# Moving the second parts of the weights by 64 bytes, and the inputs and gated products to other places, in a two-layer decoder trunk

## The chip, the cores and the metric

The kernel runs on one core of one Trainium2 chip. The metric is the device time of one execution in microseconds (us), as the median of several runs.

## What is computed

The reference is a trunk of two layers over 256 tokens of width 1024, in float32. Each layer adds half a gated feed-forward block (hidden width 2816), a token mixer, and half a second feed-forward block; each block first normalizes its input. The mixer of layer 0 is a pair of gated convolutions, that of layer 1 is attention.

```
x = x + 0.5 * swiglu_ffn(rms_norm(x, ffn1_norm[l]), ffn1_w_gate_up[l], ffn1_w_down[l])
h = rms_norm(x, mix_norm[l])
x = x + (conv_mixers(h, ...) if l % 2 == 0 else dilated_attention(h, ...))
x = x + 0.5 * swiglu_ffn(rms_norm(x, ffn2_norm[l]), ffn2_w_gate_up[l], ffn2_w_down[l])
...
swiglu_ffn: gate, up = split(x @ w_gate_up);  (silu(gate) * up) @ w_down
```

## The kernel before

All activations are kept transposed: 128 channels on the partitions, 256 tokens along the row. The weights come in *units* of 16 tiles of 128x128 float32 (1 MB) in the order of use, into four buffers `raw` of 8 KB a partition (`load`, L111). For more precision than one fast pass gives, each unit is split in two parts (`split`, L117): ScalarE rounds it into `w1` (L126), VectorE subtracts and leaves the rest in `w2` (L127), both in the fast float32 format (`float32r`). `w1` and `w2` have four buffers each. Activations are split in the same way (`split_to`, L183): a normalized input block `xs[:, d]` or a gated product `gs[:, f]` is a first part of 256 columns and a second part of 256 columns.

A tile's product is then formed in one of two ways. `mm2` (L166) issues two matmuls, called a *pair* here: `w1` against both parts at once (512 columns, L168), then `w2` against the first part (256 columns, L169). `mm3` (L158) issues three matmuls of 256 columns, called a *triple* (L162 to L164). Each matmul first loads its own 128x128 weight tile into TensorE.

The work runs in stages, in program order: for each of the four feed-forward blocks 22 gate-up units (`project2`, L324, or `project`, L314; line L375 or L377 of `ffn`), whose results are scaled, gated and split into `gs` (L381 to L388), and then the down products (L400, L402), eight output blocks of 22 tiles; between them the convolution (L422) or the attention (L578). In the feed-forward blocks nearly all tiles take pairs; the last gate-up unit, a few first ones (`ONES`) and the last output block take triples. The convolution and the attention's values and output take triples, the attention's queries and keys pairs. `Norm.add` (L287) writes the next stage's `xs` block by block as the output blocks are finished.

**Places.** A place is an address within a partition, modulo 1024 (`LINE`). A gap at L97 lets the tiles of the pool `keep` begin at a multiple of 1024, and all of `raw`, `w1` and `w2` follow at multiples of 1024. A 128x128 tile takes 512 bytes of a row, so a weight tile begins at place 0 or 512. The moving operand begins at a place that two constants set: `XS_START` for `xs` (288 in both feed-forward blocks of layer 0, 32 in those of layer 1, 192 in the convolution, 256 in the attention) and `GS_START` for `gs` (its tile begins at place 256, in the last block 320, so that 800 and 736 both give place 32). The attention's `o1` begins at place 256. Within `xs` and `gs` the two parts of a block lie side by side, 1024 bytes each, so that the 512 columns of `mm2` are one run of 2048 bytes.

Of the kernel before, what the change touches and what calls it, by code (L numbers as in the profile page):

```python
# [10 lines left out]
F32 = mybir.dt.float32  # L11
F32R = mybir.dt.float32r
# [5 lines left out]
P = 128  # L18
D = 1024
S = 256  # L20
DEPTH = 2
FF = 2816
ND = D // P
NF = FF // P
# [27 lines left out]
ONES = [4, 0, 0, 2]  # L52
ONE_END = 1
PRIO_F = 0
FFN_STEP = 40
# [4 lines left out]
WIDEC = 0  # L60
LINE = 1024
BASE = 16512
XS_START = {"F1": (288, 32), "MX": (192, 256), "F2": (288, 32)}
GS_START = (800, 800, 800, 736)
GROUPS = ((0, 2), (2, 4), (4, 6), (6, 8))
M_POOL = [0, 0, 0, 0]
B_POOL = [0, 0]
# [10 lines left out]
C_F1, C_MX, C_F2, C_FN = 0, DEPTH * ND, 2 * DEPTH * ND, 3 * DEPTH * ND  # L78
# [15 lines left out]
def trunk(ctx: ExitStack, tc: tile.TileContext, xin, wst, cst, bia, idn, out):  # L94
    nc = tc.nc
    keep = ctx.enter_context(tc.tile_pool(name="keep", bufs=1))
    keep.tile([P, (LINE - BASE % LINE) // 4], F32, name="gap")  # L97
    raws = ctx.enter_context(tc.tile_pool(name="raws", bufs=RAWS))
    w1s = ctx.enter_context(tc.tile_pool(name="w1s", bufs=WS))
    w2s = ctx.enter_context(tc.tile_pool(name="w2s", bufs=WS))  # L100
    tmp = ctx.enter_context(tc.tile_pool(name="tmp", bufs=2))
    psa = ctx.enter_context(tc.tile_pool(name="psa", bufs=4, space=PSUM))
    psb = ctx.enter_context(tc.tile_pool(name="psb", bufs=4, space=PSUM))
# [5 lines left out]
    at = {"load": 0, "split": 0}  # L109
# [20 lines left out]
    def advance(u, ahead_split=ahead_split):  # L130
        while at["load"] < min(n_units, u + ahead_load):
            load(at["load"])
            at["load"] += 1
        while at["split"] < min(n_units, u + ahead_split):
            split(at["split"])
            at["split"] += 1
# [3 lines left out]
    whole = {0} | {first_conv + i for i in WHOLE}  # L140

    class Stream:
        def __init__(self, u):
            self.u = u
# [8 lines left out]
    def take(n):  # L153
        st = Stream(used[0])
        used[0] += n
        return st

    def mm3(o, a, b, start, stop, check=False):  # L158
        if len(a) == 1:
            nc.tensor.matmul(o, a[0], b[-1], start=start, stop=stop, skip_group_check=check)  # L160
            return
        nc.tensor.matmul(o, a[0], b[0], start=start, stop=False, skip_group_check=check)  # L162
        nc.tensor.matmul(o, a[0], b[1], start=False, stop=False, skip_group_check=check)  # L163
        nc.tensor.matmul(o, a[1], b[0], start=False, stop=stop, skip_group_check=check)  # L164

    def mm2(o, w, b, start, stop):  # L166

        nc.tensor.matmul(o, w[0], b, start=start, stop=False, skip_group_check=True)  # L168
        nc.tensor.matmul(o[:, 0], w[1], b[:, 0], start=False, stop=stop, skip_group_check=True)  # L169


    x = keep.tile([P, ND, S], F32, name="x")
    xs_all = keep.tile([P, ND * 2 * S + LINE // 4], F32R, name="xs")
    const_all = keep.tile([P, LINE // 4], F32, name="const")
    const = const_all[:, :NCONST]
    ident = keep.tile([P, P], F32, name="ident")
# [6 lines left out]
    def split_to(o1, o2, src, scale=None):  # L183

        if scale is None:
            nc.scalar.copy(o1, src)
            nc.vector.tensor_sub(o2, src, o1.bitcast(F32))
        else:
            nc.scalar.activation(o1, src, AF.Copy, scale=scale)  # L189
            nc.vector.scalar_tensor_tensor(o2, src, scale, o1.bitcast(F32),  # L190
                                           op0=ALU.mult, op1=ALU.subtract)
# [86 lines left out]
    class Norm:  # L278


        def __init__(self, col, whole=None, start=0):
            self.col, self.whole = col, whole
            self.xs = xs_all[:, start // 4:start // 4 + ND * 2 * S].rearrange(
                "p (d t s) -> p d t s", d=ND, t=2)
            self.sums = tmp.tile([P, S], F32, name="sums")

        def add(self, d):  # L287
# [23 lines left out]
    def twice(r):  # L311
        return r[:, None, :].to_broadcast([P, 2, S])

    def project(st, base, xs, xg=None):  # L314

        bank = psa.tile([P, 2, S], F32, name="pa")
        for i in range(2):
            for k in range(ND):
                w = st.tile(base + 2 * k + i)
                b = (xs[:, k, 0], xs[:, k, 1]) if len(w) == 2 else (xg[:, k],)  # L320
                mm3(bank[:, i], w, b, k == 0, k == ND - 1)
        return bank

    def project2(st, base, xs):  # L324

        banks = []
        for i in range(2):
            bank = psa.tile([P, 2, S], F32, name="pa")
            for k in range(ND):
                mm2(bank, st.tile(base + 2 * k + i), xs[:, k], k == 0, k == ND - 1)  # L330
            banks.append(bank)
        return banks

    def join(v, banks, r):

        for i, bank in enumerate(banks):
            h = tmp.tile([P, S], F32, name="sq")
            nc.scalar.copy(h, bank[:, 1])  # L338
            nc.vector.tensor_add(v[:, i], bank[:, 0], h)  # L339
        nc.vector.tensor_mul(v, v, twice(r))  # L340
# [23 lines left out]
    def ffn(norm, after, between=None, first=None):  # L364
        _, r = norm.end(True, first is None)
        with tc.tile_pool(name="gp", bufs=1, reuse_waits="tile") as gp:
            st = take(NF)
            start = GS_START[st.u // FFN_STEP] // 4
            gs = gp.tile([P, NF * 2 * S + start], F32R, name="gs")[:, start:].rearrange(
                "p (f t s) -> p f t s", f=NF, t=2)  # L370
            for p in range(NF):
                advance(st.u + p)
                one = p < ONES[st.u // FFN_STEP] or p >= NF - ONE_END
                if one:
                    bank = first if first and p == 0 else project(st, p * UT, norm.xs)  # L375
                else:
                    banks = project2(st, p * UT, norm.xs)  # L377
                with tc.high_priority(offset=PRIO_F):
                    v = tmp.tile([P, 2, S], F32, name="v")
                    if one:  # L380
                        nc.vector.tensor_mul(v, bank, twice(r))  # L381
                    else:
                        join(v, banks, r)
                    sl = tmp.tile([P, S], F32, name="sl")
                    nc.scalar.activation(sl, v[:, 0], AF.Silu)  # L385
                    g = tmp.tile([P, S], F32, name="g")
                    nc.vector.tensor_mul(g, sl, v[:, 1])
                    split_to(gs[:, p, 0], gs[:, p, 1], g)  # L388
            if between:
                between(gs[:, NF - 1, 0, :1].bitcast(F32))  # L390
            st = take(NF * ND // UT)
            for d in range(ND):
                acc = psb.tile([P, 2, S], F32, name="pb")
                two = d < ND - 1
                for f in range(NF):
                    t = d * NF + f
                    if t % UT == 0 or f == 0:
                        advance(st.u + t // UT)
                    if two:
                        mm2(acc, st.tile(t), gs[:, f], f == 0, f == NF - 1)  # L400
                    else:
                        mm3(acc[:, 0], st.tile(t), (gs[:, f, 0], gs[:, f, 1]), f == 0, f == NF - 1)  # L402
                for i in range(2 if two else 1):
                    nc.vector.scalar_tensor_tensor(x[:, d], acc[:, i], 0.5, x[:, d],  # L404
                                                   op0=ALU.mult, op1=ALU.add)
                after.add(d)

    def out_half(st, accs, half, o, ds, ahead=(ahead_split,) * 2):

        for d in ds:  # L410
            for k in range(4):
                t = half * 32 + d * 4 + k
                if t % UT == 0:
                    advance(st.u + t // UT, ahead[t // UT % 2])
                mm3(accs[d // 2][:, d % 2], st.tile(t), [a[:, k] for a in o],
                    half == 0 and k == 0 and d % 2 == 0, half == 1 and k == 3, True)
# [290 lines left out]
    cold = psb.tile([P, P], F32, name="pb")  # L707
    for _ in range(WARM):
        nc.tensor.matmul(cold, ones, ones, start=True, stop=True)
    norm = Norm(C_F1, start=XS_START["F1"][0])  # L710
    for layer in range(DEPTH):
        nxt = Norm(C_MX + layer * ND, start=XS_START["MX"][layer])
        if layer == 0:
            ffn_first(norm, nxt)
        else:
            ffn(norm, nxt)
        norm, nxt = nxt, Norm(C_F2 + layer * ND, start=XS_START["F2"][layer])
        (conv if layer % 2 == 0 else attention)(norm, nxt)
        if layer < DEPTH - 1:
            norm, nxt = nxt, Norm(C_F1 + (layer + 1) * ND, start=XS_START["F1"][layer + 1])  # L720
            ffn(norm, nxt)
            norm = nxt
    with tc.tile_pool(name="fp", bufs=1, reuse_waits="tile") as fp:
# [7 lines left out]
        for i, (lo, hi) in enumerate(GROUPS):  # L731
            n = hi - lo
# [93 lines left out]
```

## Time and profile before

| | |
|---|---|
| median of 3 runs | 960.75 us (959.98 to 960.87) |
| the profiled execution | 960.66 us |
| its span, first to last instruction | 958.9 us |
| TensorE matmuls busy | 945.5 us, 99% of the span |
| VectorE busy | 724.3 us, 76% |
| ScalarE busy | 543.3 us, 57% |
| DMA | 176.24 MB, mean 184 GB/s |
| mean granted TensorE clock | 0.997 |

The span is the time from the first to the last instruction in the trace; the execution's own time holds 1.8 us more. Matmuls are pipelined, and the trace's duration of one runs on while the next has begun; what the stream of matmuls costs is read from the distance between their starts.

### The profile page before, as it was taken

How to read it: one execution, taken by the hardware profiler on the slowest of the kernel's cores; microseconds unless marked ns; L12 is line 12 of the kernel's file. 1: busy time of each engine (PE TensorE's matmuls, PEld its weight loads, DVE VectorE, ACT ScalarE, POOL GpSimd, SP SyncE). 2: the span in 40 equal slices, each digit the busy share in tenths (PEclk: the TensorE clock that was granted, in tenths of full speed). 3: DMA queues.
4: the chain of work that ended last, by engine and by line, in shares of the span. 5: the costliest groups of instructions: out<-in, count | busy, mean ns of one | idle time of the engine just before them, and what ended most of it. 6: DMA issues, size and time to landing. Idle time of an engine off the chain costs nothing.

```text
span 958.9 us, 15090 instructions
## 1 busy us (share of the span) xinstructions
PE 945.5 (99%) x5828; PEld 845.8 (88%) x5828; DVE 724.3 (76%) x1373; ACT 543.3 (57%) x975; POOL 47.1 (5%) x61
## 2 busy tenths in 40 slices
PE   8999999999999999999999999999999999999996
PEld 7988898999888888988988889898888998889886
DVE  7988866688879878766788877665698798788552
ACT  6666554488265565554466565444676565665541
POOL 0000000049600000000000000000000000000000
PEclk9999999999999999999999999999999999999998
DMA  8855555544176555555455555555553455555501
GB/s 328 291 205 192 178 206 189 178 159 148 45 260 213 193 207 181 180 211 181 176 194 202 176 191 205 178 195 212 195 191 129 149 186 194 194 202 177 194 26 44
DMA packets 27287, 176.24 MB, mean 184 GB/s; under 512 B 3024, under 2 KB 3792, under 8 KB 6864
## 3 DMA queue, kind: packets, MB, share of 16 engines
q1 hardware_dynamic: 26784, 174.67, 51.7%
q8 instruction: 45, 0.74, 0.3%
q10 hardware_dynamic: 432, 0.63, 0.2%
q14 instruction: 26, 0.21, 0.1%
HBM read 174.23 MB, written 1.05 MB: 183 GB/s over the span
## 4 chain that ended last, share of the span: by engine, by line
PE 90%; POOL 3%; DVE 3%; ACT 1%; DMA 1%; issue 1%; SPq 0%; DVEq 0%; POOLq 0%; ACTq 0%
PE pa L168 33%; PE pa L169 17%; PE pb L168 15%; PE pb L169 8%; PE pa L162 4%; PE pa L163 3%; PE pa L164 3%; POOL yp L486 3%; PE pa L160 2%; PE pb L162 1%; PE pb L163 1%; PE pb L164 1%; DVE pb L463 1%; PE pa L352 1%; PE pb L652 1%
## 5 line engine op out<-in xcount | busy, mean ns | idle before, releaser
L127 DVE TENSOR_TENSOR w<-raw,w 128x1024 fp32r<-128x1024 f32 (+1 forms) x316 | 377.0, 1205 | 136.3 <-ACT w L126 135.9
L168 PE MATMUL pa<-xs,w 128*128 128x512 f32 x1376 | 479.4, 391 | 0.1
L126 ACT CAST w<-raw 128x1024 fp32r<-128x1024 f32 (+1 forms) x316 | 320.5, 1032 | 133.5 <-PE pa L168 49.7
L169 PE MATMUL pa<-xs,w 128*128 128x256 f32 x1376 | 387.2, 282 | 0.0
L168 PEld LDWEIGHTS pa<-xs,w 128*128 128x128 f32 x1376 | 258.1, 188 | 54.9 <-DVE xs L190 0.7
L169 PEld LDWEIGHTS pa<-xs,w 128*128 128x128 f32 x1376 | 260.0, 189 | 0.3
L168 PE MATMUL pb<-gs,w 128*128 128x512 f32 x616 | 213.7, 390 | 0.0
L169 PE MATMUL pb<-gs,w 128*128 128x256 f32 x616 | 173.7, 282 | 0.0
L168 PEld LDWEIGHTS pb<-gs,w 128*128 128x128 f32 x616 | 115.6, 188 | 24.1
L169 PEld LDWEIGHTS pb<-gs,w 128*128 128x128 f32 x616 | 116.4, 189 | 0.0
L385 ACT ACTIVATE sl<-v 128x256 f32<-128x256 f32 x88 | 36.8, 418 | 108.7 <-DVE v L340 104.3
L338 ACT COPY sq<-pa 128x256 f32<-128x256 f32 x172 | 62.9, 366 | 28.6 <-PE pa L169 26.1
L163 PE MATMUL pa<-xs,w 128*128 128x256 f32 x272 | 76.3, 281 | 0.1
L162 PE MATMUL pa<-xs,w 128*128 128x256 f32 x272 | 76.3, 282 | 0.0
L164 PE MATMUL pa<-xs,w 128*128 128x256 f32 x272 | 76.2, 281 | 0.0
L339 DVE TENSOR_TENSOR v<-pa,sq 128x256 f32<-128x256 f32 x156 | 65.5, 420 | 0.0
L404 DVE SCALAR_TENSOR_TENSOR x<-pb,x 128x256 f32<-128x256 f32 x60 | 25.4, 423 | 42.5 <-PE pb L169 28.5
L189 ACT ACTIVATE xs<-x,const 128x256 fp32r<-128x256 f32 x48 | 24.3, 506 | 55.2 <-DVE x L404 43.1
L486 POOL TENSOR_TENSOR yp<-yp,prod 128x256 f32<-128x256 f32 x55 | 45.1, 822 | 208.8 <-ACT prod L485 204.8
L340 DVE TENSOR_TENSOR v<-v,rr 128x512 f32<-128x512 f32 x78 | 53.6, 688 | 0.0
L162 PEld LDWEIGHTS pa<-xs,w 128*128 128x128 f32 x272 | 51.4, 190 | 0.3
L163 PEld LDWEIGHTS pa<-xs,w 128*128 128x128 f32 x272 | 51.1, 188 | 0.5 <-DVE xs L190 0.3
(155 smaller groups left out, 900.7 us busy)
## 6 DMA issues: line engine op xcount, KB each, us to landing
raw<-wst SPq DMA_DIRECT2D x159, 1024.0 KB, 4.8
bt<-bia SPq DMA_DIRECT2D x8, 384.0 KB, 3.3
raw<-wst SPq DMA_DIRECT2D x7, 256.0 KB, 6.3
raw<-wst SPq DMA_DIRECT2D x2, 512.0 KB, 5.6
x<-xin SPq DMA_DIRECT2D x3, 256.0 KB, 5.7
out<-y SPq DMA_DIRECT2D x2, 256.0 KB, 2.5
out<-y ACTq DMA_DIRECT2D x2, 256.0 KB, 2.4
x<-xin SPq DMA_DIRECT2D x2, 128.0 KB, 3.2
```

Of the source, the lines that this page charges most:

```text
L126: nc.scalar.copy(w1[u][:, c], raw[u][:, c])
L127: nc.vector.tensor_sub(w2[u][:, c], raw[u][:, c], w1[u][:, c].bitcast(F32))
L162: nc.tensor.matmul(o, a[0], b[0], start=start, stop=False, skip_group_check=check)
L163: nc.tensor.matmul(o, a[0], b[1], start=False, stop=False, skip_group_check=check)
L164: nc.tensor.matmul(o, a[1], b[0], start=False, stop=stop, skip_group_check=check)
L168: nc.tensor.matmul(o, w[0], b, start=start, stop=False, skip_group_check=True)
L169: nc.tensor.matmul(o[:, 0], w[1], b[:, 0], start=False, stop=stop, skip_group_check=True)
L338: nc.scalar.copy(h, bank[:, 1])
L339: nc.vector.tensor_add(v[:, i], bank[:, 0], h)
L340: nc.vector.tensor_mul(v, v, twice(r))
L385: nc.scalar.activation(sl, v[:, 0], AF.Silu)
L486: nc.gpsimd.tensor_add(yp[:, c], yp[:, c], t)
```

## The change

The buffers of `w2` begin 64 bytes past a multiple of 1024, through a gap of 64 bytes before them and one of 960 after them; those of `w1` stay at multiples of 1024. `xs` and `gs` are laid out by a new function `blocks`: all first parts one after the other, then all second parts, each series beginning at a place that is given (the first number of each pair for the first parts, the second for the second parts; they are equal throughout). The tile `xs` grows by 2048 bytes. The places are

| | before | after |
|---|---|---|
| `xs`, feed-forward 1, layers 0 and 1 | 288, 32 | 288, 0 |
| `xs`, convolution, attention | 192, 256 | 192, 256 |
| `xs`, feed-forward 2, layers 0 and 1 | 288, 32 | 16, 192 |
| `gs`, the four feed-forward blocks in order | 32, 32, 32, 32 | 32, 304, 128, 64 |
| `w1` tiles | 0 or 512 | 0 or 512 |
| `w2` tiles | 0 or 512 | 64 or 576 |

`THREE` is empty, so the conditions that use it are what they were. The number, kind and order of the operations in the source are unchanged.

```diff
-XS_START = {"F1": (288, 32), "MX": (192, 256), "F2": (288, 32)}
-GS_START = (800, 800, 800, 736)
+XS_AT = {'F1': ((288, 288), (0, 0)), 'MX': ((192, 192), (256, 256)), 'F2': ((16, 16), (192, 192))}
+GS_AT = ((32, 32), (304, 304), (128, 128), (64, 64))
+GS_BASE = (256, 256, 256, 320)
+THREE = ()
+W_GAP = 64
...
     w1s = ctx.enter_context(tc.tile_pool(name="w1s", bufs=WS))
+    gaps = [ctx.enter_context(tc.tile_pool(name="gap1", bufs=1))]
+    gaps[0].tile([P, W_GAP // 4], F32, name="gap")
     w2s = ctx.enter_context(tc.tile_pool(name="w2s", bufs=WS))
+    gaps.append(ctx.enter_context(tc.tile_pool(name="gap2", bufs=1)))
+    gaps[1].tile([P, (LINE - W_GAP) // 4], F32, name="gap")
...
+    def blocks(t, base, at, n):
+        lo = (at[0] - base) % LINE
+        step = n * S * 4 + (at[1] - at[0]) % LINE
+        a = t[:, lo // 4:(lo + 2 * step) // 4].rearrange("p (t q) -> p t q", t=2)
+        return a[:, :, :n * S].rearrange("p t (k s) -> p k t s", k=n)
...
-    xs_all = keep.tile([P, ND * 2 * S + LINE // 4], F32R, name="xs")
+    xs_all = keep.tile([P, ND * 2 * S + 3 * LINE // 4], F32R, name="xs")
...
-            self.xs = xs_all[:, start // 4:start // 4 + ND * 2 * S].rearrange(
-                "p (d t s) -> p d t s", d=ND, t=2)
+            self.xs = blocks(xs_all, 0, at, ND)
...
-            start = GS_START[st.u // FFN_STEP] // 4
-            gs = gp.tile([P, NF * 2 * S + start], F32R, name="gs")[:, start:].rearrange(
-                "p (f t s) -> p f t s", f=NF, t=2)
+            n = st.u // FFN_STEP
+            gs = blocks(gp.tile([P, NF * 2 * S + 3 * LINE // 4], F32R, name="gs"), GS_BASE[n],
+                        GS_AT[n], NF)
...
-                two = d < ND - 1
+                two = d < ND - 1 and n not in THREE
```

## Rows read from the trace of the kernel before

**Rows 1.** The page's head, busy times, and chain by engine and by line.

```profile
span 958.9 us, 15090 instructions
...
PE 945.5 (99%) x5828; PEld 845.8 (88%) x5828; DVE 724.3 (76%) x1373; ACT 543.3 (57%) x975; POOL 47.1 (5%) x61
...
PE 90%; POOL 3%; DVE 3%; ACT 1%; DMA 1%; issue 1%; SPq 0%; DVEq 0%; POOLq 0%; ACTq 0%
```

**Rows 2.** Busy time in two stretches (us), all engines: gate-up, layer 1; down, layer 0.

```profile
480.00:580.00 100.00, 100.00 (x579) 88.64 (x578) 81.56 (x131) 61.05 (x110) 0.00 (x0) 1.00 0.55 191
410.00:460.00 50.00, 50.00 (x290) 44.34 (x290) 31.55 (x44) 23.09 (x31) 0.00 (x0) 1.00 0.54 190
```

**Rows 3.** Line L168 in single windows: durations ns min/median/max, first and last start.

```profile
L168 PE MATMUL pa<-xs,w x289: 390/390/390, 479.9 to 579.8; 128*128 128x512 f32 x145
L168 PE MATMUL pb<-gs,w x145: 390/390/391, 410.0 to 459.9; 128*128 128x512 f32 x145
```

**Rows 4.** Groups by line and form: the pairs' and triples' counts.

```profile
L168 PE MATMUL pa<-xs,w 128*128 128x512 f32 x1376 | 479.4, 391 | 0.1
L168 PE MATMUL pb<-gs,w 128*128 128x512 f32 x616 | 213.7, 390 | 0.0
L163 PE MATMUL pa<-xs,w 128*128 128x256 f32 x272 | 76.3, 281 | 0.1
L163 PE MATMUL pb<-gs,w 128*128 128x256 f32 x88 | 24.5, 279 | 0.0
L163 PE MATMUL pa<-o,w 128*128 128x256 f32 x64 | 18.4, 288 | 0.0
```

**Rows 5.** Timeline of weight loads and matmuls, gate-up of layer 0.

```profile
100.08 0.39 PE L168 MATMUL pa<-xs,w 128*128 128x512 f32 x1
100.08 0.19 PEld L169 LDWEIGHTS pa<-xs,w 128*128 128x128 f32 x1
100.31 0.28 PE L169 MATMUL pa<-xs,w 128*128 128x256 f32 x1
```

**Rows 6.** Timeline, first and last L162 of three series: down, convolution, attention output.

```profile
460.57 0.28 PE L162 MATMUL pb<-gs,w 128*128 128x256 f32 x1
467.92 0.28 PE L162 MATMUL pb<-gs,w 128*128 128x256 f32 x1
228.27 0.28 PE L162 MATMUL pa<-xs,w 128*128 128x256 f32 x1
231.80 0.28 PE L162 MATMUL pa<-xs,w 128*128 128x256 f32 x1
751.98 0.28 PE L162 MATMUL pa<-o,w 128*128 128x256 f32 x1
755.94 0.28 PE L162 MATMUL pa<-o,w 128*128 128x256 f32 x1
```

**Rows 7.** Timeline, L168 in two steps of the attention's queries and keys.

```profile
687.50 0.40 PE L168 MATMUL pa<-xs,w 128*128 128x512 f32 x1
692.45 0.40 PE L168 MATMUL pa<-xs,w 128*128 128x512 f32 x1
704.41 0.39 PE L168 MATMUL pa<-xs,w 128*128 128x512 f32 x1
707.53 0.39 PE L168 MATMUL pa<-xs,w 128*128 128x512 f32 x1
```

**Rows 8.** Groups by line and form: VectorE over 1024, 512 and 256 columns.

```profile
L127 DVE TENSOR_TENSOR w<-raw,w 128x1024 fp32r<-128x1024 f32 x304 | 368.4, 1223 | 133.6 <-ACT w L126 133.2
L340 DVE TENSOR_TENSOR v<-v,rr 128x512 f32<-128x512 f32 x78 | 53.6, 688 | 0.0
L187 DVE TENSOR_TENSOR gs<-g,gs 128x256 fp32r<-128x256 f32 x88 | 36.8, 419 | 0.0
```

**Rows 9.** Timeline, layer 1: the first down matmul, the last gated product's second part.

```profile
590.90 0.39 PE L168 MATMUL pb<-gs,w 128*128 128x512 f32 x1
595.03 0.42 DVE L187 TENSOR_TENSOR gs<-g,gs 128x256 fp32r<-128x256 f32 x1
```

More of the change, by code (lines that the diff above doesn't have):

```diff
@@ L278, in trunk, with __init__ @@
     class Norm:
-        def __init__(self, col, whole=None, start=0):
+        def __init__(self, col, whole=None, at=(0, 0)):
             self.col, self.whole = col, whole
-            self.xs = xs_all[:, start // 4:start // 4 + ND * 2 * S].rearrange(
-                "p (d t s) -> p d t s", d=ND, t=2)
+            self.xs = blocks(xs_all, 0, at, ND)
             self.sums = tmp.tile([P, S], F32, name="sums")
@@ L367, in ffn @@
             st = take(NF)
-            start = GS_START[st.u // FFN_STEP] // 4
-            gs = gp.tile([P, NF * 2 * S + start], F32R, name="gs")[:, start:].rearrange(
-                "p (f t s) -> p f t s", f=NF, t=2)
+            n = st.u // FFN_STEP
+            gs = blocks(gp.tile([P, NF * 2 * S + 3 * LINE // 4], F32R, name="gs"), GS_BASE[n],
+                        GS_AT[n], NF)
             for p in range(NF):
                 advance(st.u + p)
-                one = p < ONES[st.u // FFN_STEP] or p >= NF - ONE_END
+                one = n in THREE or p < ONES[n] or p >= NF - ONE_END
                 if one:
@@ L709, in trunk @@
         nc.tensor.matmul(cold, ones, ones, start=True, stop=True)
-    norm = Norm(C_F1, start=XS_START["F1"][0])
+    norm = Norm(C_F1, at=XS_AT["F1"][0])
     for layer in range(DEPTH):
-        nxt = Norm(C_MX + layer * ND, start=XS_START["MX"][layer])
+        nxt = Norm(C_MX + layer * ND, at=XS_AT["MX"][layer])
         if layer == 0:
@@ L716, in trunk @@
             ffn(norm, nxt)
-        norm, nxt = nxt, Norm(C_F2 + layer * ND, start=XS_START["F2"][layer])
+        norm, nxt = nxt, Norm(C_F2 + layer * ND, at=XS_AT["F2"][layer])
         (conv if layer % 2 == 0 else attention)(norm, nxt)
         if layer < DEPTH - 1:
-            norm, nxt = nxt, Norm(C_F1 + (layer + 1) * ND, start=XS_START["F1"][layer + 1])
+            norm, nxt = nxt, Norm(C_F1 + (layer + 1) * ND, at=XS_AT["F1"][layer + 1])
             ffn(norm, nxt)
```

## The prediction

> **What bounds the kernel now.** Look first at the page's head and its chain of waits: matmuls are busy for 99% of the span, and 90% of the chain that ends last is TensorE [rows 1]. The busy share alone says little, because a matmul's recorded duration (390 ns) runs on under the next one; what counts is the distance between starts. So look next at the busy times of a long stretch of gate-up and one of down: no idle TensorE time, a granted clock of 1.00 (the upper of its two levels, 2.4 GHz), VectorE busy for 81.56 of 100 us, ScalarE for 61.05, DMA for 0.55 of its share [rows 2]. Nothing feeds TensorE too slowly there. The stream of matmuls sets the time by itself.
>
> Its pace is read from the first and last start of line L168 in those windows: (579.8 - 479.9) / 288 = 0.3469 us from pair to pair in gate-up, (459.9 - 410.0) / 144 = 0.3465 us in down [rows 3]. I call it 346.7 ns. There are 1376 + 616 = 1992 pairs [rows 4], so 1992 x 346.7 ns = 690.6 us of the span of 958.9 us are pairs at this pace, some 72%. A change that moves the pair by 1 ns moves the time by 2.0 us. The triples are 272 + 88 + 64 = 424.
>
> The last view is the timeline inside a pair: the 512-column matmul starts, the load of the next weight tile starts with it, and the 256-column matmul follows after 0.23 us, which leaves about 0.117 us for that one [rows 5]. So **each weight load reads its 512 bytes of a row while the matmul before it reads its moving operand**. The change touches only this: at which places the two read.
>
> **What the trace says of places.** Triples are the same three instructions of the same sizes in three stages. With `gs` at place 32 a triple takes (467.92 - 460.57) / 21 = 350.0 ns, with `xs` at 192 (231.80 - 228.27) / 10 = 353.0 ns, with `o1` at 256 (755.94 - 751.98) / 11 = 360.0 ns [rows 6]. The weights are at 0 or 512 each time. That is 116.7, 117.7 and 120.0 ns a matmul: a spread of 3.3 ns that goes with the place, though the trace alone can't exclude what else differs between the stages. Pairs show the same size of step in another way: in the attention, with `xs` at 256, one step runs at (692.45 - 687.50) / 14 = 353.6 ns a pair and another at (707.53 - 704.41) / 9 = 346.7 ns [rows 7]. The pace of a pair thus has two observed levels 6.9 ns apart, 3.4 ns a matmul, and at 256 the place alone doesn't choose between them.
>
> **The change part by part.**
>
> *The second parts of the weights 64 bytes on.* No instruction is added or taken away. In a pair, one load of two (that of `w2`, under the 512-column matmul) is at a new distance from the moving operand. The load of `w1`, under the 256-column matmul, keeps its distance wherever `xs` or `gs` keeps its place. The trace has no load at a distance of 64 from the others. Bounds from the nearest rows: a gain or a loss of one level for the whole pair, 6.9 ns x 1992 = 13.7 us either way [rows 4, 7]; nothing in the rows excludes either sign. I take half a level, 3.4 ns of one matmul in each pair, as a gain: 1992 x 3.4 = 6.8 us less. The sign comes from the series of triples, in which the pace falls as the distance from the weights' place falls (360.0 at 256, 353.0 at 192, 350.0 at 32 [rows 6]); moving the load towards the operand shortens that distance where it is positive, as at 288, 304, 192, 128 and 256. Where it becomes negative (places 0, 16, 32), no row tells, and I carry the same value over. This is the weakest step.
>
> *Other places of inputs and gated products.* The feed-forward stages that move are the gate-up of the second (288 to 16), third (32 to 0) and last block (32 to 192), and the down of the second to fourth (32 to 304, 128, 64). The trace has 288 and 32 side by side only in pairs, at the same recorded durations of 390 ns; 192 and 256 only in triples or in the attention. The nearest triples bound it at 0 to +1.0 ns a matmul (32 to 192) and +3.3 ns at the worst (256) [rows 6]; a gain is not excluded, since neither 0 nor 64 is measured. Value: 0.
>
> *Two runs instead of one.* The 512 columns of a pair's first matmul become two runs of 256, 8 KB apart in `xs` and 22 KB in `gs`. No row has a matmul of two runs. Below, it costs nothing, if the pattern's second dimension is free. Above, it is like two matmuls of 256: 2 x 116.7 = 233.4 ns instead of 346.7 - 117 = 229.7, so 3.7 ns x 1992 = 7.4 us [rows 3, 4, 6]. I take 0, as no new weights are loaded between the two runs.
>
> *Triples.* 424 at a level's share of at most 3.3 ns a matmul: 424 x 3 x 3.3 = 4.2 us either way, taken as 0, for in a triple only one load of three moves.
>
> *The splitting on VectorE and ScalarE.* `w2` is now written at another place than `raw` and `w1` are read at. VectorE takes 1223 ns for 1024 columns, 688 for 512, 419 for 256 [rows 8]: 535 ns for the upper 512 columns and 269 for 256, the same 1.05 ns a column whatever is read and written. So no price of equal places is there to be saved. Were the new place dearer by 10%, VectorE would add some 122 ns to each of about 36 splits in 100 us, 4.4 us on 81.56 [rows 2]: hidden under TensorE. The cover would go only if VectorE passed 100.
>
> *Sum.* -6.8 us and zeros, from the profiled execution's own 960.66 us (span 958.9 and 1.8 around it, 0.09 below the median): 953.9 us, say **954**. A faster pair is not given back: at 343.3 ns, VectorE's 81.56 becomes 82.4 in 100 us, and DMA has half its share left [rows 2].
>
> **The rivals.**
>
> *Nothing changes, 960.7 us.* The loads and the moving operand don't disturb each other, and the spread in the triples comes from the stages. For it: at places 288 and 32 the pairs have equal recorded durations. Against it: 350.0 and 360.0 for the same instructions at the same clock [rows 6]. The Trainium skill's page "TensorE: Matmul & The Clock Gate", in "Part 2: What happens when you issue a matmul", has a rule on this side: TensorE has two independent read ports, so that loading the next weights takes no read bandwidth from the running matmul. By that rule the whole change is worth 0 and the sum is 960.7. The triples bear it out only if a cause other than place is found for them.
>
> *Both loads gain, 947 us.* If the new distance puts the pair one full level lower, it is 13.7 us: 960.66 - 13.7 = 947.0. For it: a level is the step that the pairs show [rows 7]. Against it: only one load of two moves, and no row has pairs below 346.
>
> *The slow level in the feed-forward blocks, 974 us.* If `w2` at 64 brings the attention's 353.6 ns into all pairs, it is 1992 x 6.9 = 13.7 us more: 974.4; with half of the stages, 967.5. It decides from a third of the pairs on: 664 x 6.9 = 4.6 us lost there cancel 1328 x 3.4 = 4.5 us gained on the others. For it: the level exists [rows 7]. Against it: the long stretches at 32 hold 346.7 over 288 pairs without a slip [rows 3].
>
> *A wait at the four down stages, 979 us.* The first down matmul starts at 590.90, while the last gated product's second part is written until 595.03 + 0.42 = 595.45 [rows 9]. It may start because it reads only block 0. Its operand now spans from block 0's first part across all other first parts to block 0's second part. If the wait that is set for it covers this whole span, TensorE idles for 4.55 us at each of four starts: 18.2 us, 978.9. Behind the waiting matmul stands the whole queue of TensorE. Against it: what it reads overlaps nothing that is still to be written.
>
> **How the numbers follow.** Half a level faster (954, its own range 950 to 958): 0.42. A full level (947): 0.20. Nothing: 0.19. The slow level in part or all (967 to 974): 0.14. The wait: 0.05. Faster by over 0.2% (1.9 us, about what a measurement of this kernel can tell from no change): 0.42 + 0.20 = 0.62; within it 0.19; slower 0.14 + 0.05 = 0.19. The range from 945 to 966 takes in both gains with 2 us of slack, no change, and the two runs at their upper price on top of half a level (954 + 7 = 961) or most of it on top of no gain (968); it leaves out most of the slow level and the wait, about 0.18.
>
> **What would show it.** Right: the distance of L168's starts in the same two kinds of stretch falls from 346.7 to about 343, the 512-column matmul alone being shorter (below 0.23 us), with VectorE's 1223 ns unchanged. The rivals: 340 for the full level, 346.7 for nothing, 353 for the slow one; for the wait, idle TensorE time of 4.5 us ahead of the first L168 on `gs`, released by L187. The prediction is wrong in its cause if the time falls while pairs keep 346.7, or if the 256-column matmul is the one that changes in a stage whose `xs` keeps its place (the first gate-up, at 288).

## The result, and the profile after

The changed kernel takes 967.39 us (966.55 to 967.74 over three runs), against 960.75: a ratio of 1.0062, 95% interval 1.0044 to 1.0080. It is slower by 0.6%, where 954 and faster had been forecast. The profiled execution took 967.74 us, with this head, busy times and chain (from the page):

```profile
span 966.0 us, 15090 instructions
...
PE 952.1 (99%) x5828; PEld 845.6 (88%) x5828; DVE 723.8 (75%) x1373; ACT 543.1 (56%) x975; POOL 47.1 (5%) x61
...
PE 92%; ACT 3%; DVE 2%; POOL 1%; DMA 1%; issue 0%; SPq 0%; DVEq 0%; POOLq 0%; ACTq 0%
```

As in [rows 1] TensorE fills the span, with the same number of instructions. The two long stretches, gate-up of layer 1 and down of layer 0, read like [rows 2]: no idle time, the granted clock 1.00, the other engines about as busy as before.

```profile
485.00:585.00 100.00, 100.00 (x578) 88.41 (x578) 80.61 (x130) 61.09 (x111) 0.00 (x0) 1.00 0.57 197
415.00:465.00 50.00, 50.00 (x289) 43.74 (x289) 31.22 (x43) 22.88 (x31) 0.00 (x0) 1.00 0.55 188
```

No new wait explains the time: the matmuls themselves take longer. The groups by line and form say which (L183 is L168 of before, L184 is L169, L134 is L127):

```profile
L183 PE MATMUL pa<-xs,w 128*128 128x512 f32 x1376 | 482.5, 394 | 0.0
L184 PE MATMUL pa<-xs,w 128*128 128x256 f32 x1376 | 385.3, 280 | 0.0
L183 PE MATMUL pb<-gs,w 128*128 128x512 f32 x616 | 215.6, 394 | 0.0
L134 DVE TENSOR_TENSOR w<-raw,w 128x1024 fp32r<-128x1024 f32 x304 | 367.8, 1221 | 138.8 <-ACT w L133 138.3
```

The 512-column matmul's mean goes from 391 and 390 to 394 ns [rows 4]; VectorE's split stays where it was, 1221 against 1223 ns [rows 8]. A mean over all stages hides the pattern, which appears stage by stage. Here is line L183 in one window for each of the eight feed-forward stages, in order, and last the attention (count, duration min/median/max in ns, first and last start in us; the count at the end of a row is that of a sample):

```profile
L183 PE MATMUL pa<-xs,w x257: 389/393/398, 34.7 to 124.0; 128*128 128x512 f32 x129
L183 PE MATMUL pb<-gs,w x154: 389/393/397, 132.1 to 185.5; 128*128 128x512 f32 x154
L183 PE MATMUL pa<-xs,w x287: 390/394/400, 299.7 to 399.7; 128*128 128x512 f32 x144
L183 PE MATMUL pb<-gs,w x153: 393/397/403, 409.3 to 463.0; 128*128 128x512 f32 x153
L183 PE MATMUL pa<-xs,w x289: 391/392/393, 484.8 to 584.7; 128*128 128x512 f32 x145
L183 PE MATMUL pb<-gs,w x154: 391/392/394, 594.1 to 647.2; 128*128 128x512 f32 x154
L183 PE MATMUL pa<-xs,w x284: 392/392/393, 784.8 to 884.8; 128*128 128x512 f32 x142
L183 PE MATMUL pb<-gs,w x154: 393/395/396, 893.0 to 946.5; 128*128 128x512 f32 x154
L183 PE MATMUL pa<-xs,w x127: 391/392/498, 678.9 to 734.8; 128*128 128x512 f32 x127
```

Last minus first start, over the count less one, is the pace of a pair: (884.8 - 784.8) / 283 = 353 ns in the seventh line, (584.7 - 484.8) / 288 = 347 in the fifth. The table takes the same from the trace's starts in nanoseconds, over the pairs alone and with those that hold a stall left out, as sums of the mean distance behind the 512-column matmul and that behind the 256-column one. The paces that the expectations below quote differ from these by up to 0.7 ns.

| stage | pairs | place before, after | ns a pair before | after | us |
|---|---|---|---|---|---|
| gate-up 1 | 272 | 288, 288 | 228.4 + 118.3 = 346.7 | 230.9 + 118.0 = 348.9 | +0.6 |
| down 1 | 154 | 32, 32 | 228.3 + 118.3 = 346.7 | 230.8 + 118.1 = 348.9 | +0.3 |
| gate-up 2 | 336 | 288, 16 | 228.5 + 118.3 = 346.8 | 232.3 + 117.7 = 350.0 | +1.1 |
| down 2 | 154 | 32, 304 | 228.3 + 118.3 = 346.7 | 232.6 + 120.8 = 353.3 | +1.0 |
| gate-up 3 | 336 | 32, 0 | 228.4 + 118.3 = 346.7 | 229.7 + 117.1 = 346.7 | 0.0 |
| down 3 | 154 | 32, 128 | 228.3 + 118.3 = 346.7 | 229.6 + 117.1 = 346.7 | 0.0 |
| gate-up 4 | 304 | 32, 192 | 228.4 + 118.3 = 346.7 | 231.7 + 121.6 = 353.3 | +2.0 |
| down 4 | 154 | 32, 64 | 228.3 + 118.3 = 346.7 | 232.0 + 118.0 = 350.0 | +0.5 |
| attention | 128 | 256, 256 | 234.2 + 116.5 = 350.8 | 229.6 + 117.1 = 346.7 | -0.5 |

The pairs make +5.1 us of the 6.6 (sums are rounded). The attention's 96 value matmuls of 512 columns go from 227.5 to 232.2 ns, +0.5 us, and the 424 triples, by their starts, add some +0.7 us; the rest is within the spread of the runs. The first two stages are the telling ones: their places did not move, so only the gap acts there, and only on the matmul under which `w2` is loaded.

The wait that was feared at the down stages isn't there. The timeline at the third down has its first matmul on `gs` right behind the last gate-up matmul, as in [rows 9]:

```profile
594.03 0.28 PE L179 MATMUL pa<-xs,w 128*128 128x256 f32 x1
594.15 0.39 PE L183 MATMUL pb<-gs,w 128*128 128x512 f32 x1
```

### The profile page after: what moved, and what is told of

It reads as the page before. It is cut to its first block, busy times and chain, and to the rows that moved or that the text cites. A ratio compares the mean times of both kernels' runs of the same rounds, so it can differ in the third digit from the quotient of the medians.

```text
span 966.0 us, 15090 instructions
## 1 busy us (share of the span) xinstructions
PE 952.1 (99%) x5828; PEld 845.6 (88%) x5828; DVE 723.8 (75%) x1373; ACT 543.1 (56%) x975; POOL 47.1 (5%) x61
## 4 chain that ended last, share of the span: by engine, by line
PE 92%; ACT 3%; DVE 2%; POOL 1%; DMA 1%; issue 0%; SPq 0%; DVEq 0%; POOLq 0%; ACTq 0%
PE pa L183 33%; PE pa L184 17%; PE pb L183 15%; PE pb L184 8%; PE pa L177 4%; PE pa L179 4%; PE pa L178 4%; PE pa L175 3%; ACT prod L499 2%; PE pb L177 1%; PE pb L178 1%; PE pb L179 1%; DVE pb L477 1%; POOL yp L500 1%; ACT w L133 1%; PE pb L666 1%
## 5 line engine op out<-in xcount | busy, mean ns | idle before, releaser
L183 PE MATMUL pa<-xs,w 128*128 128x512 f32 x1376 | 482.5, 394 | 0.0
L134 DVE TENSOR_TENSOR w<-raw,w 128x1024 fp32r<-128x1024 f32 (+1 forms) x316 | 376.4, 1203 | 141.6 <-ACT w L133 141.1
L184 PE MATMUL pa<-xs,w 128*128 128x256 f32 x1376 | 385.3, 280 | 0.0
L183 PEld LDWEIGHTS pa<-xs,w 128*128 128x128 f32 x1376 | 258.3, 188 | 58.6 <-DVE xs L205 0.4
L184 PEld LDWEIGHTS pa<-xs,w 128*128 128x128 f32 x1376 | 259.2, 188 | 0.2
L183 PE MATMUL pb<-gs,w 128*128 128x512 f32 x616 | 215.6, 394 | 0.0
L184 PE MATMUL pb<-gs,w 128*128 128x256 f32 x616 | 173.0, 281 | 0.0
L183 PEld LDWEIGHTS pb<-gs,w 128*128 128x128 f32 x616 | 116.0, 188 | 26.6
L184 PEld LDWEIGHTS pb<-gs,w 128*128 128x128 f32 x616 | 115.7, 188 | 0.0
L178 PE MATMUL pa<-xs,w 128*128 128x256 f32 x272 | 76.6, 282 | 0.0
L178 PEld LDWEIGHTS pa<-xs,w 128*128 128x128 f32 x272 | 51.2, 188 | 0.4 <-DVE xs L205 0.2
```

Of the source, the lines that this page charges most:

```text
L134: nc.vector.tensor_sub(w2[u][:, c], raw[u][:, c], w1[u][:, c].bitcast(F32))
```

## The experiments

Sixteen runs followed: twelve kernels derived from the changed one, and four repeats. A ratio is that to the kernel before, timed beside it on the same chip; where none is given the kernel ran once. *Distance* is the place of the moving operand less that of the weight tile (0 for `w1`, the gap for `w2`).

**1 to 4: the change taken apart.** Each edit is against the changed kernel.

e1_layout, the layout alone:

```diff
-    ...gap1, gap2...
-XS_AT = {... (288, 288), (0, 0) ... (16, 16), (192, 192)}
+XS_AT = {... (288, 288), (32, 32) ... (288, 288), (32, 32)}
-GS_AT = ((32, 32), (304, 304), (128, 128), (64, 64))
+GS_AT = ((32, 32), (32, 32), (32, 32), (32, 32))
```

> The new layout in two runs (all first parts, then all second parts), with every place as in the kernel before and no gap: weights at 0 or 512, xs at 288, 192, 288, 32, 256, 32, gs at 32. Theory (the pace of the pairs follows the places alone): as the kernel before, 346.7 ns a pair in all feed-forward stages, 960.7 us, within 1 us. Rival (the 512 columns in two runs cost something): the 512-column matmul goes from 228 ns up by up to 3.7 ns in every stage, the time to between 962 and 968 us.

Measured: 960.58 us, ratio 0.9993 (0.9985 to 1.0002). The 512 columns in two runs cost nothing; every feed-forward stage runs at 346.7 to 346.8 ns, as the window of the third gate-up shows, which is [rows 3] again (L178 is L168):

```profile
L178 PE MATMUL pa<-xs,w x290: 390/390/390, 479.7 to 579.9; 128*128 128x512 f32 x145
```

e2_gap, the same with the gap of 64 kept:

```diff
-XS_AT, GS_AT of the change
+XS_AT, GS_AT of e1_layout
```

> The new layout and the 64 bytes before the second parts of the weights, with xs and gs at the places of before. Theory: the first gate-up (288) and the first down (32) of the changed kernel, whose places did not move, ran at 349.0 ns a pair, so all eight feed-forward stages run at 349.0 here, 2.3 ns x 1864 pairs = 4.3 us more than before, while the attention's pairs gain 4 ns x 128 = 0.5 us as in the changed kernel: about 964.5 us. Rival (the gap is harmless, the new places of xs and gs cost all): 960.7 us.

Measured: 965.35 us, ratio 1.0045 (1.0033 to 1.0058). All eight feed-forward stages run at 348.9 ns, 230.8 + 118.1: the whole loss sits in the matmul under which `w2` is loaded. Third gate-up, and second down:

```profile
L183 PE MATMUL pa<-xs,w x287: 389/393/397, 479.9 to 579.7; 128*128 128x512 f32 x144
L183 PE MATMUL pb<-gs,w x153: 389/393/397, 410.6 to 463.6; 128*128 128x512 f32 x153
```

(579.7 - 479.9) / 286 = 349 against 347 of e1: the expectation holds in size, stage and matmul, and the rival falls. The 230.8 is a mean: from pair to pair the distance behind this matmul is 226, 231 and 235 ns in turn, through each of the eight stages, where it was 228 or 229 almost throughout before. The attention gained less than expected (348.5, though its places and gap are those of the changed kernel, which had 346.7).

One rival is VectorE, which now writes `w2` at another place while TensorE reads. Its share differs between the two windows, 81% in the gate-up and 63% in the down:

```profile
480.00:580.00 100.00, 100.00 (x575) 87.58 (x575) 81.21 (x138) 59.66 (x109) 0.00 (x0) 1.00 0.54 186
411.00:461.00 50.00, 50.00 (x289) 43.81 (x288) 31.56 (x45) 23.52 (x33) 0.00 (x0) 1.00 0.55 192
```

The pace is 348.9 ns in both, so it doesn't follow VectorE's load.

e3_places, the new places without the gap:

```diff
-    ...gap1, gap2...
```

> The new layout and the new places of xs and gs, without the gap (second parts of the weights at 0 or 512 like the first). Theory that only the distance between a weight load and the moving operand counts: the first gate-up, the first down and the attention, whose places are those of before, return to 346.7 ns a pair (346.7 to 353 in the attention); the others take a pace of their own, not that of the changed kernel, as each load of w2 is 64 bytes nearer. If gap and places added up, the time would be 960.7 + (967.4 - 964.5) = 963.6 us. Rival (the gap alone costs): 960.7 us.

Measured: 965.84 us, ratio 1.0048 (1.0036 to 1.0061). The places alone cost as much as the gap alone, and the two together (1.0062) cost less than their sum: they don't add up, because each decides what the other does. First gate-up and first down are back at 346.7. At gap 0 the place 128 takes 351.0 ns, where at gap 64 it took 346.7; 304 takes 349.9 instead of 353.3, and 64 takes 353.2 instead of 350.0; 192 takes 353.2 and 16 takes 346.9. The rows are the fourth gate-up (192) and the third down (128):

```profile
L178 PE MATMUL pa<-xs,w x284: 397/397/398, 784.8 to 884.8; 128*128 128x512 f32 x142
L178 PE MATMUL pb<-gs,w x152: 387/396/400, 593.9 to 646.9; 128*128 128x512 f32 x152
```

One thing fits no theory of the places: the convolution, whose places are those of e1_layout, ran its triples at 341.9 ns here (113.7 + 113.8 + 114.4) and at 352.2 there. In equal windows of 23 us, the second matmul of a triple, first e1_layout, then e3_places:

```profile
L173 PE MATMUL pa<-xs,w x66: 281/281/281, 220.9 to 243.9; 128*128 128x256 f32 x66
...
L173 PE MATMUL pa<-xs,w x68: 276/276/276, 221.0 to 243.8; 128*128 128x256 f32 x68
```

e4_shift, every distance of before at another place:

```diff
+    ...gap1 ahead of w1s, so that w1 and w2 both begin at 64...
+XS_AT = {'F1': ((352, 352), (96, 96)), 'MX': ((256, 256), (320, 320)), 'F2': ((352, 352), (96, 96))}
+GS_AT = ((96, 96), (96, 96), (96, 96), (96, 96))
```

> Both parts of the weights 64 bytes past a multiple of 1024, and xs and gs 64 bytes further than in the kernel before (352, 96, 256, 320; gs 96): every distance between a weight load in the split format and the moving xs or gs is that of before, every place is another. Theory (distance counts): 346.7 ns a pair in all feed-forward stages, 960.7 us within 1 us. Rival (the place itself counts, as that of xs against something that didn't move with it): paces between 347 and 353 ns as at the other places of the changed kernel, 963 to 973 us.

Measured: 960.70 us, ratio 0.9993 (0.9984 to 1.0002). The paces of all eight feed-forward stages come back to within 0.1 ns of the kernel before: with this shift at least, the distance between the weight load and the moving operand counts, not the place. Third gate-up and second down, beside [rows 3]:

```profile
L183 PE MATMUL pa<-xs,w x290: 390/390/390, 479.6 to 579.8; 128*128 128x512 f32 x145
L183 PE MATMUL pb<-gs,w x154: 390/390/390, 410.7 to 463.8; 128*128 128x512 f32 x154
```

The attention's `o1` stayed at 256 and so changed its distance: its triples went from 120 to 115 ns a matmul.

**5 to 8: sweeps.** Four kernels with other gaps and a place of its own for each stage.

```diff
 e5_sweep0:   (no gap)     gate-ups 80, 112, 96, 144;  downs 160, 176, 208, 224
 e6_sweep32:  W_GAP = 32   gate-ups 0, 48, 32, 16;     downs 64, 96, 160, 224
 e7_sweep128: W_GAP = 128  gate-ups 0, 64, 32, 96;     downs 128, 160, 192, 224
 e8_sweep96:  W_GAP = 96   gate-ups 0, 64, 32, 96;     downs 128, 160, 192, 224
```

> A sweep of places in one run, both parts of the weights at 0 or 512 (no gap), new layout: gate-ups at 80, 112, 96, 144, downs at 160, 176, 208, 224, convolution and attention at 32. Theory (distance between a weight load and the moving operand counts, and repeats after 256 bytes, since 32 and 288 gave the same): each stage has a pace of its own between 346 and 354 ns a pair; at 144 to 224, next to 128 and 192 (350.9 and 353.1), above 350. Rival 1 (346.5 ns is a floor that nothing goes under): no stage below 346. Rival 2 (a better distance exists, since the triples of the convolution fell to 342 ns in one run): at least one stage at 343 or less.

> The same sweep with a gap of 32 bytes: gate-ups at 0, 48, 32, 16, downs at 64, 96, 160, 224, convolution and attention at 0. Theory: the two loads of a pair have distances 32 apart, paces between those at gap 0 and at gap 64 for the same places: 346 to 350 at 0, 16 and 32, above 349 at 64 and above. Rival 1 (floor): no stage below 346. Rival 2: one at 343 or less.

> The same sweep with a gap of 128 bytes: gate-ups at 0, 64, 32, 96, downs at 128, 160, 192, 224, convolution and attention at 128. Theory: at gap 64 the places 0, 128 and 256 gave 346.8, so each load has some distances that cost nothing; a stage is at the floor where both of its loads have such a distance, which a gap of 128 gives at other places than 64. Between 346 and 354. Rival 1 (floor): no stage below 346. Rival 2: one at 343 or less.

> The same sweep with a gap of 96 bytes: gate-ups at 0, 64, 32, 96, downs at 128, 160, 192, 224, convolution at 160, attention at 0. Theory: as at gap 128, between 346 and 354 by place. Rival 1 (floor): no stage below 346. Rival 2: one at 343 or less.

Measured (967.32, 963.23, 967.20 and 966.30 us, one run each), with the paces of the runs above filled in, ns a pair:

| place | gap 0 | gap 32 | gap 64 | gap 96 | gap 128 |
|---|---|---|---|---|---|
| 0 | 346.8 | 346.7 | 346.7 | 351.7 | 346.7 |
| 16 | 346.9 | 344.6 | 350.0 | | |
| 32 | 346.7 | 344.5 | 348.9 | 346.7 | 346.7 |
| 64 | 353.2 | 348.9 | 350.0 | 346.7 | 346.8 |
| 96 | 350.0 | 353.2 | | 349.3 | 350.0 |
| 128 | 351.0 | | 346.7 | 346.7 | 352.0 |
| 160 | 346.7 | 350.7 | | 348.4 | 350.0 |
| 192 | 353.2 | | 353.3 | 353.2 | 353.2 |
| 224 | 346.7 | 348.4 | | 353.3 | 350.7 |

There is no simple rule in it. The range of 346 to 354 held in e5, e7 and e8, but the finer expectations failed. In e5 all places from 144 to 224 were to be above 350: 144, 160 and 224 ran at 346.7, 176 at 350.0, and only 208, with 353.3, was above. In e6, 16 and 32 were to be at 346 or more and ran at 344.6 and 344.5, and 64 and 224, expected above 349, ran at 348.9 and 348.4. The floor fell: 344.5 and 344.6 at gap 32 are under every feed-forward pace of before, yet none of the four runs reached the 343 of the second rival. Each cell is mostly one stage of one execution, and the runs below show that some distances have two paces.

**9 to 11: the best point.**

e9_gap32:

```diff
-W_GAP = 64
+W_GAP = 32
+XS_AT: 32 in all feed-forward stages and the attention, 192 in the convolution; GS_AT: 32
```

> A gap of 32 bytes instead of 64, and xs and gs at 32 in all feed-forward stages and the attention (192 in the convolution). In the sweep with that gap the gate-up at 32 ran at 344.5 ns a pair. Theory (the distance sets the pace, whatever the stage): 344.5 in all eight stages, 2.0 ns x 1864 pairs = 3.7 us less than before, and some 6 ns x 128 = 0.8 us in the attention: 956.3 us. Rival (a pace belongs to a stage and to how its stream happened to start): between 344.5 and 349 by stage, 957 to 963 us.

Measured: 959.27 us, ratio 0.9983 (0.9974 to 0.9992): faster than the kernel before, if only by 0.17%, and not the 956.3 of the theory. The rival came closer: three gate-ups and the last down ran at 344.5 to 344.7 ns, the fourth gate-up and the other downs at 346.7 to 346.8, at the same two distances.

e10_near and e11_second:

```diff
 W_GAP = 32
-XS_AT, GS_AT of e9_gap32
+e10_near:   gate-ups 288, 20, 24, 28;  downs 40, 16, 32, 24
+e11_second: first parts at 32; second parts: gate-ups 160, 224, 96, 288;  downs 64, 160, 0, 192
```

> The neighbourhood of that point, gap 32: gate-ups at 288, 20, 24, 28, downs at 40, 16, 32, 24, convolution at 32, attention at 16. Theory (distance, repeating after 256 bytes): 288 as 32, 344.5; 16 as in the sweep, 344.8; the places between them 344 to 346, 40 towards the 348.8 of 48. Rival (the pace belongs to the stage): 288 and 32 differ by more than 1 ns.

> Gap 32, first parts of xs and gs at 32, second parts elsewhere: gate-ups 160, 224, 96, 288, downs 64, 160, 0, 192. The second part is read only by the second half of the 512-column matmul, after the load under it has been going for over 100 ns. Theory (a load meets only the first columns of the matmul above it): 344.5 in all stages, as with equal places. Rival (it also meets the second run): paces by place between 344 and 354.

Measured in e10 (972.70 us): 288 gave 344.5 and 16 gave 344.5; the 32 of the third down gave 346.7, as that stage had in e9, so the rival's difference between 288 and 32 is there, as one of the two paces of e9. But 40 gave 359.7, 20 gave 360.0, 24 gave 356.7 twice, the worst paces of the study, and 28 gave 346.7. That was not expected. First down (40) and third gate-up (24):

```profile
L183 PE MATMUL pb<-gs,w x154: 396/403/403, 130.9 to 186.0; 128*128 128x512 f32 x154
L183 PE MATMUL pa<-xs,w x281: 396/399/405, 479.8 to 579.7; 128*128 128x512 f32 x141
```

Measured in e11 (965.69 us): 350.0, 346.7, 353.2 and 346.7 in the gate-ups, 350.0, 350.0, 350.0 and 346.9 in the downs. The theory that a load meets only the first columns of the matmul above it falls: the second run's place moves the pace by up to 9 ns (353.2 with it at 96, against 344.5 in the same stage of e9 with it at 32).

**12: the gap of 64 at the places that bore it.** In e12_gap64_places, `xs` is at 0 or 128, `gs` at 128:

```diff
+XS_AT = {'F1': ((0, 0), (0, 0)), ... 'F2': ((128, 128), (128, 128))}
+GS_AT = ((128, 128), (128, 128), (128, 128), (128, 128))
```

> The gap of 64 bytes as in the changed kernel, but xs at 0 in the first and third gate-up and at 128 in the second and fourth, gs at 128 in all four downs (convolution and attention as in the changed kernel). In the changed kernel the only feed-forward stages at the pace of before, 346.8 ns a pair, were the gate-up at 0 and the down at 128. Theory (the two distances decide, and 128 repeats 0 for this gap): 346.8 in all eight stages, the loss of the changed kernel gone: 960.7 us, within 1.5 us. Rival 1 (the gap itself costs in most stages, whatever the place): paces near 349, 964 to 965 us. Rival 2 (one distance can run at two paces, as 32 did with the gap of 32): some stages at 346.8 and others not.

Measured: 961.78 us, ratio 1.0005 (0.9995 to 1.0015). The loss of the changed kernel is gone with the gap still in place, so the gap is dear only together with the places. In the profiled execution (963.73 us) six stages ran at 346.7, and the last two, at 128 like four others, at 353.3: the second rival has a part in it.

**13 to 16: does the program fix the pace?** Four kernels again, unaltered: the changed one, the one before, e12 and e9.

> The changed kernel again, unaltered, for a second profile. Theory (the program fixes the pace of each stage): the same paces, 349.0, 349.0, 350.2, 353.1, 346.8, 346.8, 352.7, 349.6 ns a pair in the eight feed-forward stages, each within 0.3 ns. Rival (the execution chooses between two paces): some of them, 353.1 and 352.7 above all, come out lower by 3 to 7 ns or others higher.

> The kernel before again, unaltered. Theory: 346.3 to 346.7 ns in all feed-forward stages, and the attention's steps at 353 and 346.7 in the same order. Rival: the attention's steps, or a feed-forward stage, at another pace.

> The kernel of the gap of 64 with places 0 and 128 again. Theory: 346.7 in six feed-forward stages and 353.0 in the last gate-up and the last down. Rival: the last two at 346.7 too, or 353.0 elsewhere.

> The kernel of the gap of 32 again. Theory: 344.5 in the first three gate-ups and the last down, 346.8 in the others, as in the first profile. Rival: another order of the two.

The changed kernel (966.23 us) repeats its eight paces to 0.1 ns: 348.9, 348.9, 350.0, 353.3, 346.8, 346.7, 353.3, 350.0. The kernel before (960.31 us) does too, 346.7 to 346.8, and 350.8 in the attention. So the table of the result is no chance. The other two differ in few stages. e15 (960.72 us) has its last gate-up and last down at 346.7; the 304 + 154 pairs of these, at 6.6 ns, are the 3.0 us that it is below e12's profiled 963.73. e16 (958.91 us) has the fourth gate-up at 344.5 and the last down at 346.8, the reverse of e9. The fourth gate-up in e12, e15, e9 and e16, one row of each:

```profile
L183 PE MATMUL pa<-xs,w x280: 397/397/397, 784.7 to 883.2; 128*128 128x512 f32 x140
...
L183 PE MATMUL pa<-xs,w x280: 391/392/393, 784.9 to 881.6; 128*128 128x512 f32 x140
...
L183 PE MATMUL pa<-xs,w x274: 391/391/391, 784.7 to 879.4; 128*128 128x512 f32 x137
...
L183 PE MATMUL pa<-xs,w x275: 387/389/389, 784.8 to 879.1; 128*128 128x512 f32 x138
```

The durations are almost constant within each row: in these runs a stage takes one of two paces and keeps it to its end. For some distances an execution may fall into the one or the other; for those of the changed kernel and the kernel before no feed-forward stage did, in two profiles each.

## Why the prediction was wrong

**The bound was right.** TensorE's stream of matmuls sets the time, its pace is read from the distance of starts, and the change acts only through where a weight load and the moving operand read. e4_shift shows that this interaction exists and goes by distance: with these distances restored and the places of `w1`, `w2`, `xs` and `gs` all changed, the time was that of before. The prediction had this only as an argument from triples in different stages.

**The step that failed is "the second parts of the weights 64 bytes on".** It was priced at half a level as a gain, -3.4 ns of one matmul in each pair, -6.8 us. e2_gap measured +2.4 ns (228.4 to 230.8) on that one matmul, in every feed-forward stage, and 4.8 us more than e1_layout. The matmul and the order of size were right, the sign was not. The sign came from a series of three points in triples (32, 192, 256), read as "less distance, less time". The trace of before had a fourth point that breaks it: the triples at the end of the first gate-up read `xs` at 288, which the prediction took to be there only in pairs. The first and last L162 of these sixteen are

```profile
125.73 0.28 PE L162 MATMUL pa<-xs,w 128*128 128x256 f32 x1
130.98 0.28 PE L162 MATMUL pa<-xs,w 128*128 128x256 f32 x1
```

(130.98 - 125.73) / 15 = 350.0 ns, at the longest distance the pace of the shortest. The sweep shows for pairs too that there is no such slope: at gap 0 the pace is 346.7 at 32, 353.2 at 64, 351.0 at 128, 346.7 at 160, 353.2 at 192. Three stages with one place each can't carry a direction, and the bounds, which excluded neither sign, should have carried the forecast.

**"Other places" was valued at 0** and was worth as much as the gap: e3_places costs 0.48% without it. On top of the gap, by the paces of the pairs in the two traces, it is 1.3 us: the second down at 304 and the fourth gate-up at 192 (353.3 ns each) lose 2.0, the third gate-up and the third down win back 1.0, the other stages make the rest. The prediction treated gap and places as separate terms; each load sees their difference, so they aren't.

**The other terms held.** Two runs: 0 (0.9985 to 1.0002 in e1). The split on VectorE: 1221 ns. The wait: none. The triples: some +0.7 us, inside their bound of 4.2.

**The rival that came true** is the slow level, in part: the prediction gave it 967.5 "with half of the stages", against 967.39, but as a second copy of the attention's 353.6 ns. In fact two of eight stages are at 353.3, two at 350.0, two at 348.9, and two unharmed, so that the figures agree is luck. The rival that nothing changes, by the rule of the Trainium skill's page "TensorE: Matmul & The Clock Gate", section "Part 2: What happens when you issue a matmul", falls: loading weights is said to take no read bandwidth from the running matmul, while here the same instructions with other distances differ by 1.0045 (1.0033 to 1.0058) in time. The measurement decides; whether it is read bandwidth that is lost, no run shows.

What stays open: why a distance has the pace that it has, and what puts a stage into one of two paces at the same distances.

## What to carry to other kernels

Where TensorE streams float32r matmuls back to back and loads new weights for each, the start addresses of weights and moving operands against each other moved a pair between 344.5 and 360.0 ns here, and they can be swept cheaply, since each stage of one run can have a place of its own. Read the pace by stage from the first and last start, and repeat the profile before trusting a pace, for some distances have two. Don't extrapolate from a few places, and choose gap and places together: the gap of 64 bytes cost 0.45% at the old places and nothing that could be told at 0 and 128.

## What was not expected of the hardware

- The pace of a pair was the same at 32 and 288, 256 bytes apart, in three gaps: 346.7 to 346.8 ns at gap 0, 348.9 at gap 64, 344.5 at gap 32. At 0 and 256 it was the same in the changed kernel (346.7), but not at gap 0 (346.8 in a gate-up, 350.8 in the attention, where one step ran slow and another not [rows 7]).
- Many stages keep 346.7, 350.0, 353.3, 356.7 or 360.0 ns. These are 3.3 ns apart, eight periods of the 2.4 GHz at which the clock was granted. Where the mean lies between them, as 348.9 does, single pairs rotate through different distances.
- Places of the moving operand that are no multiple of 16 bytes can cost far more: 20 and 40 gave 360.0 and 359.7 ns, 24 gave 356.7, beside 344.5 at 16; yet 28 gave 346.7.
- Triples at the same distances ran at 352 and 342 ns in the convolution, in two kernels. The best triples seen, 340.0 ns or 113.3 a matmul of 256 columns, are the sixteen of e5's fourth gate-up, with `xs` at 144; nothing in these runs shows how to get such a pace reliably.
